# Retention with the value weights last: decayed scores times modulated rows, then the value projection; context keys of two heads ahead of the heads

## The chip, the cores and the metric

The kernel runs on one core of one Trainium2 chip. Its time is in device microseconds (us), the median over several executions of the same program. One more execution of each kernel was profiled; the rows and stretches below are from that one. Engines: PE is TensorE (matrix products; PEld its weight loads), DVE is VectorE, ACT is ScalarE, POOL is GpSimd, SP issues most of the DMAs. Each engine works through its own instructions strictly in program order.

## What is computed

A backbone of two layers over 256 latent tokens and 256 context tokens of width 1024. Layer 0 mixes tokens with a Fourier and neighbourhood-attention mixer, layer 1 with bidirectional retention; each layer ends in a mixture of experts. The change is in layer 1's retention, which reads (cut to what matters):

```python
xm = rmsnorm(x, g) * (1 + scale) + shift         # latent rows, "modulated"; cm the same for the context rows
q, k, v, g = split(xm @ w_in)                    # 4 heads: q and k 256 wide (k / 16, both with rotary), v and g 512 wide
kc, vc = split(cm @ w_in)                        # the context gives keys and values, without rotary
o = (decay * (q @ concat(kc, k).T)) @ concat(vc, v)     # both directions of the scan together: a full decay matrix
y = (silu(g) * rmsnorm(o)) @ w_out               # norm over the 512 columns of a head
```

With X the 512 modulated rows (context, then latent), P the decayed scores and Wv a head's value weights, a head's output is P (X Wv). It may also be computed as (P X) Wv.

## The kernel before, in words

Every float32 product is done in three products of a reduced format: each operand is split into a high part (a copy by ScalarE, names ending in hi or h) and a low part (a subtraction by VectorE, names ending in lo or l), and `mm3` (L313 to L320) adds high times high, low times high and high times low in one PSUM accumulator. Weights are split the same way: a load fills a tile `raw` (128x2048), `split` (L166 to L180) makes two `whi` on ScalarE (L176) and two `wlo` on VectorE (L178) from it. Raw tiles and pairs of whi and wlo come from two rings of slots, `raw` and `hl`; a load waits on its queue until its slot has been read. Loads go out on SP's queue, some small ones on GpSimd's.

Layer 1's retention begins in `moe0_tail`, behind the last expert of layer 0. `combine` adds the experts' sums to the residual rows `h`; `norm_scale` and `norm_mod` norm a tile of 128 rows, transpose it on TensorE (`nT`) and modulate it into `r_xc` (context) and `r_xl` (latent), features on the partitions. There the kernel loads head 0's value weights and key weights, computes the values of one context tile (`v_ps`) and the keys of the context for head 0 (`k_ps`).

`ret_heads` then goes through four heads. Per head: context keys (`k_ctx`), keys and queries of the latent tokens with rotary (`roped`, L1252 to L1254, tiles `qk_ps`, `rt`, `ro`), values of four token tiles (`v_ps`, 4 x 8 x 3 products of 512 columns), scores (`s_ps`, 24 products of 256 columns) times the decay (`pf`) and split (`ph`, `pl`), the gate (`g_ps`, 48 products of 512 columns, silu into `gt`), and the output (`ro_ps`, 2 x 4 x 3 products of 512 columns), normed and gated into `og`. Chunks of the conditioning (`ada_step`: a weight load, 64 small products into `ada_ps`, a bias into `adab`, and rows `mod` written to DRAM for later use) are spread between. Behind the heads `og` is transposed (`tsp`) and multiplied by the output weights (`ry_ps`).

The code is written in the order wanted; a scheduler then interleaves the engines' work, so that each engine's final order is not the code's.

Of the kernel before, what the change touches and what calls it, by code (L numbers as in the profile page):

```python
# [12 lines left out]
ALU = mybir.AluOpType  # L13
# [97 lines left out]
class Net:  # L111
    def __init__(self, ctx, tc, A, out, stop=None, dbg=None):
# [4 lines left out]
        self.add_slots(ctx, "raw", 4)  # L117
# [142 lines left out]
    def ada_mm(self, layer, c, aps, psp):  # L260
# [20 lines left out]
        def finish():  # L281
# [10 lines left out]
            if vec not in (SH1, SC1):  # L292
# [3 lines left out]
                for i in range(2 if layer == 0 else 1):  # L296
                    d = nc.gpsimd.dma_start(row[i, 512 * ch:512 * ch + 512].rearrange("(j p) -> j p", p=128), r[i:128:32])
# [24 lines left out]
    def norm_scale(self, t, x):  # L322
# [9 lines left out]
        return self.nc.vector.tensor_scalar(x, self.h[:, t], r, None, ALU.mult)  # L332
# [24 lines left out]
    def mixer0(self):  # L357
# [3 lines left out]
        with ExitStack() as es0:  # L361
# [142 lines left out]
            with ExitStack() as es:  # L504
# [4 lines left out]
                self.add_hl(self.ctx, 2, "right")  # L509
                self.hx = self.ctx.enter_context(ExitStack())  # L510
                self.add_raw(self.hx, 2)
# [225 lines left out]
    def moe0_tail(self, ep, psp, hps):  # L737
# [3 lines left out]
        self.kc = [xr.tile([128, 2, 256], F32R, name=f"r_kc{i}") for i in range(2)]  # L741
        self.v0 = xr.tile([128, 512], F32, name="r_v0")
# [3 lines left out]
        x = X["xg"]  # L746
        xms = lambda: ep.tile([128, 4, 128], F32, tag="g", name="xm")
        mm, add = self.combine(2)
        last = self.norm_scale(2, x[0])
# [3 lines left out]
        last = self.norm_scale(3, x[1])  # L753
        with after(last):
            self.ret_wv = wv = [self.weight(("ret_w_in", (), 4 * i, 4, 2048, 512)) for i in range(2)]
        for t in (2, 3):
            last = self.norm_mod(1, t, x[t - 2], xms, psp, *self.xc)
        with after(last):
            self.ret_w0 = w0 = self.weight(self.ret_keys(0)[0])
# [10 lines left out]
    def vproj(self, ws, x, t, ps):  # L770
        tk = slice(128 * t, 128 * t + 128)
        for k in range(8):
            self.mm3(ps, (x[0][:, k, tk], x[1][:, k, tk]), self.wk(ws[k // 4], k % 4), k == 0, k == 7)
        return ps

    def proj_t(self, w, x, ps, tk):
        for f in range(2):
# [8 lines left out]
    def k_ctx(self, w, ps, tk):  # L786
        self.proj_t(w, self.xc, ps, tk)
        self.split_scaled(self.kc[0][:, :, tk], self.kc[1][:, :, tk], ps[:, :, tk], 0.0625)
# [374 lines left out]
    def retention(self):  # L1163
        nc, A, tc = self.nc, self.A, self.tc
        h = self.h
        with ExitStack() as es:
# [4 lines left out]
            with ExitStack() as es1:  # L1171
                ogp = self.pool(es1, "r_og", 1)
                og = ogp.tile([128, 2, 2048], F32, name="og")
                with ExitStack() as es2:
# [4 lines left out]
                    self.ret_heads(wk, mmp, sp, psp, aps, xs, og)  # L1179
# [3 lines left out]
                self.hx = self.ctx.enter_context(ExitStack())  # L1183
                self.add_raw(self.hx, 3, late=True)
# [4 lines left out]
                for kc in range(4):  # L1189
                    oh, ol = xs[kc // 2]  # L1190
                    ks = slice(4 * (kc % 2), 4 * (kc % 2) + 4)
                    for t in range(2):
                        tq = slice(128 * t, 128 * t + 128)
                        self.transpose_split(og[:, t, 512 * kc:512 * kc + 512], 4, oh[:, ks, tq], ol[:, ks, tq], psp)
# [32 lines left out]
    def ret_heads(self, wk, mmp, sp, psp, aps, xs, og):  # L1227
# [5 lines left out]
        full, half = slice(0, 256), (slice(0, 64), slice(64, 128))  # L1233

        def proj(ws, t, name):
            ps = mmp.tile([128, 512], F32, tag="mm", name=name)
            tk = slice(128 * (t % 2), 128 * (t % 2) + 128)
            xhi, xlo = xs[t // 2]
            for k in range(8):
                self.mm3(ps, (xhi[:, k, tk], xlo[:, k, tk]), self.wk(ws[k // 4], k % 4), k == 0, k == 7)  # L1240
            return ps

        def weights(c0, pool=0):
            return [self.weight(("ret_w_in", (), 4 * i, 4, c0, 512), pool) for i in range(2)]
# [472 lines left out]
```

## Time and profile before

| | before |
|---|---|
| median of 3 executions | 1287.11 us (1286.89 to 1289.53) |
| profiled execution, its time | 1290.84 us |
| its span in the trace | 1289.0 us |
| TensorE busy | 1203.7 us, 93% |
| VectorE busy | 941.8 us, 73% |
| ScalarE busy | 755.6 us, 59% |

The busy shares are means over the whole program. The four heads lie between about 681 us and 909 us of the span, the norms ahead of them between about 641 us and 685 us, the start of layer 0's expert stage between about 325 us and 352 us.

### The profile page before, as it was taken

The page shows a single profiled execution, that of the slowest core. Times are in us where ns is not written, and L with a number is a line of the kernel's source. Part 1 is how long each engine was busy: PE and PEld are TensorE (multiplying, and loading weights), DVE is VectorE, ACT ScalarE, POOL GpSimd, SP SyncE. Part 2 cuts the span into 40 slices and gives each one's busy share as a digit, 9 for nine tenths or more (in the row PEclk, how much of TensorE's full clock was granted, in tenths as well). Part 3 has the DMA queues.
Part 4 walks back from the last instruction along what each step waited for, and adds up shares of the span by engine and source line. Part 5 has one row for each costly group of instructions (what it writes and reads, how often), then busy time and mean ns, then how long its engine had stood idle before and what let it go on. Part 6 is the DMA issues. An engine that isn't in the chain of part 4 may idle for free. (4 is left out here: it accounts for less than half of the span.)

```text
span 1289.0 us, 18819 instructions
## 1 busy us (share of the span) xinstructions
PE 1203.7 (93%) x7093; PEld 946.8 (73%) x7093; DVE 941.8 (73%) x1601; ACT 755.6 (59%) x1122; POOL 124.5 (10%) x126
## 2 busy tenths in 40 slices
PE   4999999898699999999979999999997999999995
PEld 3777666566588888777668888898776788877673
DVE  4755666866698989888897554554657899888985
ACT  3753555723488888778544433343435777777663
POOL 1010102300111112111000000000004000000020
PEclk8999999999799999999989999999998999999998
DMA  9666774342899999999883445432749999889980
GB/s 348 254 238 244 270 256 153 106 166 102 332 354 373 365 363 365 359 362 347 299 326 111 147 157 199 154 119 98 270 174 359 369 369 367 336 334 344 336 335 9
DMA packets 60885, 340.60 MB, mean 264 GB/s; under 512 B 10252, under 2 KB 14860, under 8 KB 24144
## 3 DMA queue, kind: packets, MB, share of 16 engines
q1 hardware_dynamic: 46656, 303.07, 62.4%
q0 software_dynamic: 11392, 31.81, 7.6%
q10 hardware_dynamic: 2736, 4.41, 1.0%
q8 instruction: 59, 0.97, 0.3%
q14 instruction: 42, 0.34, 0.1%
HBM read 333.74 MB, written 18.40 MB: 273 GB/s over the span
## 5 line engine op out<-in xcount | busy, mean ns | idle before, releaser
L178 DVE TENSOR_TENSOR wlo<-raw,whi 128x1024 fp32r<-128x1024 f32 x471 | 558.8, 1221 | 114.2 <-ACT whi L176 113.0
L176 ACT ACTIVATE whi<-raw 128x1024 fp32r<-128x1024 f32 x476 | 481.2, 1054 | 106.8 <-PE qk_ps L319 24.5
L319 PE MATMUL h_ps<-wlo,xh 128*128 128x512 f32 x512 | 208.6, 407 | 4.5 <-DVE wlo L178 4.3
L318 PE MATMUL h_ps<-whi,xh 128*128 128x512 f32 x512 | 206.1, 403 | 3.3 <-ACT xh L1457 2.4
L320 PE MATMUL h_ps<-whi,xl 128*128 128x512 f32 x512 | 206.1, 402 | 0.1
L319 PEld LDWEIGHTS h_ps<-wlo,xh 128*128 128x128 f32 x512 | 97.6, 191 | 38.4 <-DVE wlo L178 17.6
L318 PEld LDWEIGHTS h_ps<-whi,xh 128*128 128x128 f32 x512 | 97.9, 191 | 26.0 <-ACT xh L1457 2.6
L320 PEld LDWEIGHTS h_ps<-whi,xl 128*128 128x128 f32 x512 | 97.6, 191 | 21.3 <-DVE xl L675 0.7
L275 PE MATMUL ada_ps<-raw,cT 128*32 128x128 f32 x1536 | 53.8, 276 | 2.1 <-DMA raw<-in_ada_w 2.1
L319 PE MATMUL y_ps<-wlo,gh 128*128 128x512 f32 (+1 forms) x136 | 53.5, 394 | 0.4 <-DVE wlo L178 0.3
L318 PE MATMUL y_ps<-whi,gh 128*128 128x512 f32 (+1 forms) x136 | 53.0, 391 | 0.7 <-ACT gh L674 0.7
L320 PE MATMUL y_ps<-whi,gl 128*128 128x512 f32 (+1 forms) x136 | 52.6, 395 | 0.1
L275 PEld LDWEIGHTS ada_ps<-raw,cT 128*32 128x32 f32 x1536 | 41.4, 110 | 13.9 <-issue 9.2
L319 PE MATMUL y<-wlo,gh 128*128 128x512 f32 x124 | 49.1, 396 | 0.4 <-DVE wlo L178 0.3
L318 PE MATMUL y<-whi,gh 128*128 128x512 f32 x124 | 49.2, 397 | 0.2 <-ACT gh L674 0.2
L320 PE MATMUL y<-whi,gl 128*128 128x512 f32 x124 | 48.4, 400 | 0.9 <-DVE gl L675 0.8
L1104 POOL DMA_INDIRECT moe_sum<-y,tok x15 | 28.1, 1877 | 158.1 <-ACT y L1099 158.1
L674 ACT ACTIVATE gh<-tsp 128x512 fp32r<-128x512 f32 x32 | 19.1, 596 | 41.4 <-PE tsp L671 41.2
L318 PE MATMUL qk_ps<-xhi,whi 128*128 128x512 f32 x96 | 39.4, 410 | 0.0
L319 PE MATMUL qk_ps<-xlo,whi 128*128 128x512 f32 x96 | 38.7, 403 | 0.0
L320 PE MATMUL qk_ps<-xhi,wlo 128*128 128x512 f32 x96 | 38.3, 399 | 0.0
L1604 POOL DMA_INDIRECT out_dram<-hg,tok x4 | 10.6, 2638 | 268.0 <-DVE hg L1598 218.4
(441 smaller groups left out, 2391.9 us busy)
## 6 DMA issues: line engine op xcount, KB each, us to landing
raw<-in_moe_w SPq DMA_DIRECT2D x188, 1024.0 KB, 7.6
raw<-in_ada_w SPq DMA_DIRECT2D x48, 1024.0 KB, 5.3
raw<-in_ret_w_in SPq DMA_DIRECT2D x24, 1024.0 KB, 5.7
raw<-in_mixab_w_in SPq DMA_DIRECT2D x10, 1024.0 KB, 5.6
raw<-in_ret_w_out SPq DMA_DIRECT2D x8, 1024.0 KB, 4.9
raw<-in_mixab_w_out SPq DMA_DIRECT2D x4, 1024.0 KB, 8.2
raw<-in_moe_w POOLq DMA_DIRECT2D x4, 1024.0 KB, 11.0
bias<-in_rpb ACTq DMA_DIRECT2D x12, 256.0 KB, 5.6
```

The costliest lines, as they stand in the source:

```text
L176: self.nc.scalar.activation(hi, r, AF.Copy)
L178: eng.tensor_tensor(lo, r, hi.bitcast(F32), ALU.subtract)
L275: mm = nc.tensor.matmul(ps[32 * j:32 * j + 32, 0:128], self.cT[:, kk, :], raw[:, k, 128 * j:128 * j + 128], start=(kk == 0), stop=(kk == 7 ...
L318: mm(out, lh, rh, start=first, stop=False)
L319: mm(out, lh, rl, start=False, stop=False)
L320: self.mm_last = mm(out, ll, rh, start=False, stop=last)
L674: i = nc.scalar.activation(hi[:, b0:b0 + w], tv, AF.Copy)
L1104: nc.gpsimd.indirect_dma_start(out=self.F[:, :], out_offset=bass.IndirectOffsetOnAxis(ap=R["tok"][:, e:e + 1], axis=0), in_=y, in_offset=N ...
L1604: self.nc.gpsimd.indirect_dma_start(out=self.out[:, :], out_offset=bass.IndirectOffsetOnAxis(ap=idx, axis=0), in_=x, in_offset=None, bound ...
```

## The change

A head now computes Z = P X first (transposed, features on the partitions: `z_ps`, 8 blocks of 128 features x 4 token tiles x 3 products of 256 columns), splits it (`zh`, `zl`) and multiplies it by the value weights (`ro_ps`, 2 x 8 x 3 products of 512 columns). For this the modulated rows are needed with tokens on the partitions: `natural` multiplies each of the four tiles of normed rows by the scale row and adds the shift row, copies the high part (`xnh`) and subtracts for the low part. Those rows come by four broadcast loads from DRAM (`rows`), so the shift and scale of layer 1 are written to DRAM as well, by eight more small DMAs.

Around this: `moe0_tail` loads the key weights of heads 0 and 1 in place of head 0's value and key weights, and computes the context keys of head 0 and of half of head 1 (256 columns each product); the other half follows in `ret_heads` behind the latent norms. There are two sets of context keys. The gate is computed ahead of the scores and its silu goes to `og`; the next head's keys are computed between a head's scores and its Z. One conditioning chunk runs in each head (before, one in head 0's stretch of code and up to two in the others). The rings are smaller in the heads: three raw tiles and four hl pairs, where there were four and six. The fourth raw tile holds the low part of the natural context rows until the last Z.

```diff
@@ the end of a conditioning chunk
-            if vec not in (SH1, SC1):
+            if layer or vec not in (SH1, SC1):
...
-                for i in range(2 if layer == 0 else 1):
+                for i in range(2 if layer == 0 or vec in (SH1, SC1) else 1):
@@ moe0_tail
-            self.ret_wv = wv = [self.weight(("ret_w_in", (), 4 * i, 4, 2048, 512)) for i in range(2)]
+            self.ret_w0 = w = [self.weight(self.ret_keys(0)[0])]
...
-            self.ret_w0 = w0 = self.weight(self.ret_keys(0)[0])
+            w.append(self.weight(self.ret_keys(1)[0]))
...
-        v = hps.tile([128, 512], F32, tag="h", name="v_ps")
-        self.vproj(wv, self.xc, 0, v)
-        nc.scalar.copy(self.v0, v)
-        self.k_ctx(w0, hps.tile([128, 2, 256], F32, tag="h", name="k_ps"), slice(0, 256))
+        self.k_ctx(0, w[0], hps.tile([128, 2, 256], F32, tag="h", name="k_ps"))
+        self.k_ctx(1, w[1], hps.tile([128, 2, 256], F32, tag="h", name="k_ps"), (0,))
@@ ret_heads, ahead of the loop over heads
+        xnh = wk.tile([128, 4, D], F32R, name="xnh")
+        self.ring["raw"][:] = [q for q in self.ring["raw"] if q is not self.raw1]
+        xc = self.raw1.tile([128, 2, D], F32R, tag="raw", name="xnlc")
...
+        def rows(i):
+            t = self.raw_tile()
+            for j, vec in enumerate((SC1, SH1)):
+                nc.gpsimd.dma_start(t[:, 1024 * j:1024 * j + 1024],
+                                    self.modrow[1, vec][i:i + 1].partition_broadcast(128))
+            return t
+        def natural(m, x, r, tmp=None):
+            V.tensor_tensor(x, x, r[:, 0:D], ALU.mult)
+            V.tensor_tensor(x, x, r[:, D:], ALU.add)
+            nc.scalar.activation(xnh[:, m], x, AF.Copy)
+            V.tensor_tensor(xnl[m], x, xnh[:, m].bitcast(F32), ALU.subtract)
...
+        self.k_ctx(1, self.ret_w0[1], mmp.tile([128, 2, 256], F32, tag="mm", name="k_ps"), (1,))
+        kl = keys(0, self.ret_w0[0])
+        with self.tc.issue_after(last.ins):
+            r = rows(1), rows(0)
+            for m in range(4):
+                natural(m, h[:, 2 + m] if m < 2 else x[m - 2], r[m // 2])
@@ ret_heads, in a head
-                w_v = weights(2048 + 512 * hd)
-                for m in range(4):
-                    vproj(w_v, m)
+            if hd < 3:
+                w = self.weight(self.ret_keys(hd + 1)[0])
+                if hd:
+                    self.k_ctx(hd + 1, w, mmp.tile([128, 2, 256], F32, tag="mm", name="k_ps"))
+                kl = keys(hd + 1, w)
+            def z_part(i):
+                z = mmp.tile([128, 2, 256], F32, tag="mm", name="z_ps")
+                for b in range(2):
+                    cs = kcol(2 * i + b, 128)
+                    for m in range(4):
+                        self.mm3(z[:, b], (xnh[:, m, cs], xnl[m][:, cs]), (ph[:, m], pl[:, m]), m == 0, m == 3)
...
+            w_v = weights(2048 + 512 * hd)
+            o = [sp.tile([128, 512], F32, tag="s", name="ro_ps") for t in range(2)]
+            z_part(0)
+            for i in range(4):
+                if i < 3:
+                    z_part(i + 1)
+                for b in range(2):
+                    k = 2 * i + b
+                    for t in range(2):
+                        tq = kcol(t, 128)
+                        self.mm3(o[t], (zh[i][:, b, tq], zl[i][:, b, tq]), self.wk(w_v[k // 4], k % 4), k == 0, k == 7)
```

How this moves instructions is seen in each engine's order of the built program. First VectorE at head 0, before: the last split of latent rows (`r_xl`), value splits (`vl`), weight splits, and the rotary of the keys.

```order
L351 TENSOR_SCALAR og<-nT,modcol 128x128 x3
L354 TENSOR_TENSOR r_xl_13258<-og,r_xl_13257 128x4x128 x2
L1262 TENSOR_TENSOR vl<-v_ps,vh 128x512
L178 TENSOR_TENSOR wlo<-raw,whi 128x1024 x3
L1262 TENSOR_TENSOR vl<-v_ps,vh 128x512
L178 TENSOR_TENSOR wlo<-raw,whi 128x1024 x2
L1252 TENSOR_TENSOR rt<-qk_ps,ropet 64x512 x2
L1253 TENSOR_TENSOR ro<-qk_ps,ropet 128x512
L178 TENSOR_TENSOR wlo<-raw,whi 128x1024
L1254 TENSOR_TENSOR ro<-ro,rt 128x512
L178 TENSOR_TENSOR wlo<-raw,whi 128x1024
L784 SCALAR_TENSOR_TENSOR k_13447<-ro,k_13446 128x512
```

The same place now. Ahead of these rows stand the last split of latent rows, two scale operations (L1246) and two shift operations (L1247) of the context rows, one scale operation of latent rows, and the keys' rotary with two low parts (L1249) between its steps; the first `wlo` here belongs to head 0's gate weight, the last row is the queries' split.

```order
L777 SCALAR_TENSOR_TENSOR k_13402<-ro,k_13401 128x512
L1247 TENSOR_TENSOR xn<-xn,raw 128x1024
L1246 TENSOR_TENSOR xn<-xn,raw 128x1024
L1257 TENSOR_TENSOR rt<-qk_ps,ropet 64x512
L1249 TENSOR_TENSOR xnl_13284<-xn,xnh 128x1024
L1247 TENSOR_TENSOR xn<-xn,raw 128x1024
L1257 TENSOR_TENSOR rt<-qk_ps,ropet 64x512
L1258 TENSOR_TENSOR ro<-qk_ps,ropet 128x512
L1249 TENSOR_TENSOR xnl_13285<-xn,xnh 128x1024
L1259 TENSOR_TENSOR ro<-ro,rt 128x512
L180 TENSOR_TENSOR wlo<-raw,whi 128x1024
L777 SCALAR_TENSOR_TENSOR q_13483<-ro,q_13482 128x512
```

All twelve operations of `natural` (four each of L1246, L1247 and L1249) now stand between the last split of latent rows and the first split of a gate weight.

Second, GpSimd's queue at the start of layer 0's experts, before: row broadcasts and row writes of the stage ahead of it, then the gather of the first expert's rows (`xg`), four weight loads, and the second gather.

```order
L312 DMA g_3528<-mod_5_1752 128x1024
L312 DMA g_3530<-mod_5_1752 128x1024
L892 DMA xd_2322<-xm_3265 128x1024
L1713 BRANCH_PREFETCH_HINT
L1026 DMA xg_3540<-xd_2322,tok_3471 128x1024
L157 DMA raw<-in_moe_w 128x2048 x4
L1026 DMA xg_3541<-xd_2322,tok_3471 128x1024
L710 TENSOR_LOAD ovi_3512
```

The same place now:

```order
L314 DMA g_3541<-mod_5_1755 128x1024
L314 DMA g_3543<-mod_5_1755 128x1024
L887 DMA xd_2330<-xm_3273 128x1024
L1734 BRANCH_PREFETCH_HINT
L1021 DMA xg_3553<-xd_2330,tok_3479 128x1024
L299 DMA mod_0_3527<-adab 4x128 x4
L159 DMA raw<-in_moe_w 128x2048 x4
L1021 DMA xg_3554<-xd_2330,tok_3479 128x1024
L712 TENSOR_LOAD ovi_3520
L1108 COMPARE_AND_BRANCH
```

Four writes of `mod` rows (`L299`) have come between the first gather and the four weight loads.

Third, ScalarE at the end of the heads, before: silu of head 3's gate, weight copies (the `whi` there belong to the gate), the copies and squares of the output, and the copies of transposed rows for the output product.

```order
L1314 ACTIVATE gt<-g_ps 128x512
L176 ACTIVATE whi<-raw 128x1024 x3
L1314 ACTIVATE gt<-g_ps 128x512
L176 ACTIVATE whi<-raw 128x1024
L1322 COPY og<-ro_ps 128x512
L1324 ACTIVATE jk,r_ss<-og 128x512
L1322 COPY og<-ro_ps 128x512
L1324 ACTIVATE jk,r_ss<-og 128x512
L674 ACTIVATE r_xl_13257<-tsp 128x4x128 x4
L674 ACTIVATE r_oc_15400<-tsp 128x4x128 x2
```

The same place now; the two `whi` nearest to the squares (L1343) are those of the first output weights, the ones that `ry_ps` needs first.

```order
L1326 ACTIVATE zh<-z_ps 128x512 x2
L178 ACTIVATE whi<-raw 128x1024
L1326 ACTIVATE zh<-z_ps 128x512
L178 ACTIVATE whi<-raw 128x1024
L1326 ACTIVATE zh<-z_ps 128x512
L178 ACTIVATE whi<-raw 128x1024 x2
L1343 ACTIVATE jk,r_ss<-ro_ps 128x512
L178 ACTIVATE whi<-raw 128x1024
L1343 ACTIVATE jk,r_ss<-ro_ps 128x512
L676 ACTIVATE r_xl_13263<-tsp 128x4x128 x2
L178 ACTIVATE whi<-raw 128x1024
L676 ACTIVATE r_xl_13263<-tsp 128x4x128 x2
```

The copies of the output (L1322) are gone, and two weight copies stand ahead of and between the squares.

## Rows read from the trace of the kernel before

**Rows 1.** The page, part 1: busy us and share of the span.

```profile
PE 1203.7 (93%) x7093; PEld 946.8 (73%) x7093; DVE 941.8 (73%) x1601; ACT 755.6 (59%) x1122; POOL 124.5 (10%) x126
```

**Rows 2.** Windows: length, busy us PE, PEld, DVE, ACT, POOL; clock; DMA; GB/s.

```profile
700.00:740.00 40.00, 39.72 (x311) 35.66 (x310) 25.87 (x46) 15.12 (x22) 1.13 (x2) 1.00 0.40 137
...
860.00:910.00 50.00, 49.74 (x271) 41.98 (x269) 26.40 (x31) 20.58 (x27) 0.95 (x1) 1.00 0.35 123
```

**Rows 3.** Timeline of PE at the heads' start: start, duration, instruction.

```profile
662.13 0.28 PE L318 MATMUL k_ps<-r_xc,whi 128*128 128x256 f32 x1
...
665.36 0.28 PE L318 MATMUL k_ps<-r_xc,whi 128*128 128x256 f32 x1
...
668.04 1.95 PE L275 MATMUL ada_ps<-raw,cT 128*32 128x128 f32 x64
...
673.09 0.40 PE L318 MATMUL v_ps<-whi,r_xc 128*128 128x512 f32 x1
...
677.06 0.39 PE L320 MATMUL v_ps<-whi,r_xc 128*128 128x512 f32 x1
...
681.44 0.50 PE L318 MATMUL v_ps<-whi,r_xl 128*128 128x512 f32 x1
```

**Rows 4.** Tile ro_ps: ns min/median/max, first and last start us.

```profile
L320 PE MATMUL ro_ps<-vh,pl x32: 388/389/397, 719.5 to 908.6; 128*128 128x512 f32 x32
```

**Rows 5.** Tile k_ps: weight loads of its 256-column products.

```profile
L318 PEld LDWEIGHTS k_ps<-r_xc,whi x64: 187/188/192, 660.8 to 855.1; 128*128 128x128 f32 x64
```

**Rows 6.** Timeline of DVE, norms and head 0 (idle before, in brackets).

```profile
660.64 2.35 DVE L178 TENSOR_TENSOR wlo<-raw,whi 128x1024 fp32r<-128x1024 f32 x2
...
683.67 1.30 DVE L354 TENSOR_TENSOR r_xl<-og,r_xl 128x512 fp32r<-128x512 f32 x2 [0.47 <-ACT r_xl L353]
688.34 0.69 DVE L1262 TENSOR_TENSOR vl<-v_ps,vh 128x512 fp32r<-128x512 f32 x1 [3.37 <-ACT vh L1261]
...
699.84 1.39 DVE L1252 TENSOR_TENSOR rt<-qk_ps,ropet 64x512 f32<-64x512 f32 x2
```

**Rows 7.** Timeline of ACT, third pair of weight copies.

```profile
655.09 2.01 ACT L176 ACTIVATE whi<-raw 128x1024 fp32r<-128x1024 f32 x2
```

**Rows 8.** Timeline of PE, start of the first expert stage.

```profile
331.10 1.94 PE L671 MATMUL tsp<-cst,xg 128*128 128x128 f32 x8 [5.44 <-DVE mk L728]
...
348.79 0.37 PE L1018 MATMUL tbw<-wv,os 128*128 128x48 bf16 x8 [2.91 <-DVE wv L985]
```

**Rows 9.** Windows at the first expert stage, columns as rows 2.

```profile
324.00:326.00 2.00, 0.73 (x2) 0.37 (x2) 1.28 (x7) 0.66 (x2) 0.52 (x1) 0.50 0.00 0
...
332.00:336.00 4.00, 4.00 (x12) 2.70 (x11) 4.00 (x8) 3.09 (x4) 0.00 (x0) 0.51 1.02 414
336.00:340.00 4.00, 4.00 (x19) 3.24 (x18) 4.00 (x10) 2.01 (x2) 0.00 (x0) 1.00 1.01 424
```

**Rows 10.** Tile mod: the issues that write it, ns min/median/max.

```profile
L297 POOL DMA_DIRECT2D mod<-adab x24: 537/542/652, 74.4 to 974.9; - x24
```

**Rows 11.** Timeline of POOL, start of the first expert stage.

```profile
326.57 2.17 POOL L157 DMA_DIRECT2D raw<-in_moe_w  x4
```

**Rows 12.** Timeline of ACT, start of the first expert stage.

```profile
343.37 1.06 ACT L176 ACTIVATE whi<-raw 128x1024 fp32r<-128x1024 f32 x1 [4.68 <-DMA raw<-in_moe_w]
```

**Rows 13.** Timeline of SP's queue towards the end of the heads.

```profile
865.58 27.57 SPq L157 DMA_DIRECT2D raw<-in_ret_w_out  x4
```

**Rows 14.** The page, part 6: KB each, us to landing.

```profile
raw<-in_ret_w_out SPq DMA_DIRECT2D x8, 1024.0 KB, 4.9
```

**Rows 15.** Timeline of ACT at the end of the heads.

```profile
908.99 0.58 ACT L1322 COPY og<-ro_ps 128x512 f32<-128x512 f32 x1 [1.38 <-PE ro_ps L320]
909.61 0.63 ACT L1324 ACTIVATE jk<-og 128x512 f32<-128x512 f32 x1
910.14 0.19 ACT L1324 ACTIVATION_READ_ACCUMULATOR jk<-og 128x1 f32 x1
910.71 1.08 ACT L674 ACTIVATE r_xl<-tsp 128x512 fp32r<-128x512 f32 x2 [0.37 <-PE tsp L671]
```

More of the change, by code (lines that the diff above doesn't have):

```diff
@@ L320, in mm3, with norm_scale @@
         self.mm_last = mm(out, ll, rh, start=False, stop=last)
-    def norm_scale(self, t, x):
+    def norm_scale(self, t, x, out=None):
         nc = self.nc
@@ L740, in moe0_tail @@
         self.xc = [xr.tile([128, 8, 256], F32R, name=f"r_xc{i}") for i in range(2)]
-        self.kc = [xr.tile([128, 2, 256], F32R, name=f"r_kc{i}") for i in range(2)]
-        self.v0 = xr.tile([128, 512], F32, name="r_v0")
+        self.kc = [[xr.tile([128, 2, 256], F32R, name=f"r_kc{j}{i}") for i in range(2)] for j in range(2)]
         self.ada_q = [(1, c) for c in (6, 7, 8, 9)]
@@ L1233, in ret_heads, with weights @@
         full, half = slice(0, 256), (slice(0, 64), slice(64, 128))
[L1235 to L1244, printed above, removed]
+        kcol = lambda t, n=512: slice(n * t, n * t + n)
+        xnh = wk.tile([128, 4, D], F32R, name="xnh")
+        self.ring["raw"][:] = [q for q in self.ring["raw"] if q is not self.raw1]
+        xc = self.raw1.tile([128, 2, D], F32R, tag="raw", name="xnlc")
+        xnl = [xc[:, 0], xc[:, 1]] + [wk.tile([128, D], F32R, name=f"xnl{t}") for t in range(2)]
+        def weights(c0):
+            return [self.weight(("ret_w_in", (), 4 * i, 4, c0, 512)) for i in range(2)]
+        def rows(i):
[9 more added lines that the diff above has]
+            V.tensor_tensor(xnl[m], x, xnh[:, m].bitcast(F32), ALU.subtract)
         def roped(w, out, scale):
@@ new lines, in keys @@
+        def keys(hd, w):
+            kl = [wk.tile([128, 2, 256], F32R, tag=f"k{i}", name=f"k{i}") for i in range(2)]
+            roped(w, kl, 0.0625)
+            return kl
+        x = [ogp.tile([128, D], F32, tag=f"g{t}", name="xn") for t in range(2)]
+        xm = [ogp.tile([128, 2, 4, 128], F32, tag=f"g{t}", name="xm") for t in (2, 3)]
+        xm = [xm[i // 2][:, i % 2] for i in range(4)]
+        for t in range(2):
+            self.norm_scale(t, x[t])
+        for t in range(2):
+            last = self.norm_mod(1, t, x[t], lambda: xm.pop(0), psp, *xs[0])
@@ L1290, in ret_heads @@
             nc.gpsimd.dma_start(dm, self.dmat[hd].rearrange("p (m q) -> p m q", m=4))
-            if hd:
-                w_v = weights(2048 + 512 * hd)
-                for m in range(4):
-                    vproj(w_v, m)
+            ws = weights(4096 + 512 * hd)
+            ps = [mmp.tile([128, 512], F32, tag="mm", name="g_ps") for t in range(2)]
+            for k in range(8):
+                for t in range(2):
+                    tq = kcol(t, 128)
+                    self.mm3(ps[t], (xs[0][0][:, k, tq], xs[0][1][:, k, tq]), self.wk(ws[k // 4], k % 4), k == 0, k == 7)
+            og.append(ogp.tile([128, 2, 512], F32, tag=f"g{hd}", name="og"))
+            for t in range(2):
+                nc.scalar.activation(og[hd][:, t], ps[t], AF.Silu)
             ph = wk.tile([128, 4, 256], F32R, tag="ph", name="ph")
@@ L1310, in ret_heads @@
             self.ada_step(aps, psp)
-            gt = wk.tile([128, 2, 512], F32, tag="gt", name="gt")
-            ws = weights(4096 + 512 * hd)
-            for t in range(2):
-                nc.scalar.activation(gt[:, t], proj(ws, t, "g_ps"), AF.Silu)
+            if hd < 3:
[3 more added lines that the diff above has]
+                kl = keys(hd + 1, w)
+            zh, zl = [], []
```

93 lines of the change are left out of this document (34 added, 59 removed).

## The prediction, made before the changed kernel was run

> **What bounds the kernel now.** I read the engine shares first, then the stretches of the four heads, then the single engines around the start of the heads, because an average over the program says nothing of the place that the change touches. TensorE is busy for 93% of the span, VectorE for 73% [rows 1]. In the heads TensorE has no gaps to speak of: 39.72 of 40 us, and 49.74 of 50 us at their end, at the full clock, while VectorE has a third to a half of its time free [rows 2]. There a product saved on TensorE is time saved, and VectorE's extra work is free as long as TensorE has products queued that don't wait for it. At the first head that condition is what must be looked at: before it lies a chain of norms on VectorE, and TensorE gets the latent rows from that chain.
>
> **Products.** A product of 512 columns follows the one before it after (677.06 - 673.09) / 17 = 0.2335 us, one of 256 columns after (665.36 - 662.13) / 27 = 0.1196 us, a conditioning chunk takes 1.95 us [rows 3]. Per head the change takes out 96 + 24 products of 512 and adds 96 of 256 and 48 of 512: 4 x (28.0 - 22.7) = 21.3 us less. Not all of it counts. In the kernel before, head 0's context value products (48 of 512) lie inside the norm chain, where TensorE waits anyway; now context keys of head 1 lie there. So I count only what stands behind the first product on latent rows. Before: 624 x 0.2335 + 624 x 0.1196 + 3 x 1.95 = 226.2 us, from 681.44 [rows 3] to 907.6; the last product of the heads starts at 908.6 in the trace [rows 4], so the count is good to 1 us. Now: 384 x 0.2335 + 960 x 0.1196 + 4 x 1.95 = 212.3 us. **Term A: -13.9.**
>
> Two prices could spoil A. A 256-column product carries as many weight loads as one of 512, and a load takes 188 ns, longer than 0.1196 us [rows 5]. If loads set the pace, A would be 384 x 0.2335 + 960 x 0.188 + 7.8 less 624 x 0.2335 + 624 x 0.188 + 5.9, that is +9.1 us. But the 0.1196 us was measured with a load before every product, so they overlap and I take it. The Trainium skill, page "TensorE: Matmul & The Clock Gate", section "Back-to-back issue gap", says that spacing is set by load and product together, and gives about 131 ns at 512 columns and 81 ns at 128. By an estimate on the line between these, 256 columns cost 98 ns, three quarters of 512, and the change would save nothing on products; this trace, with a ratio of 0.51, differs.
>
> **Start of the heads.** The last split of latent rows ends at 683.67 + 1.30 = 684.97 [rows 6]. Ahead of it the change takes two weight copies out of ScalarE that stand between the copies of the context rows (2.01 us at 655.09, with the last two row copies behind them [rows 7]), and one pair of weight splits out of VectorE (2.35 us at 660.64 [rows 6]). I let the chain come 2.0 us earlier; bounds 0 (the row broadcasts and the second weight load share the DMA and land late) and 4 (both pairs count). Into the chain come one weight split (1.18) and the rest of the split keys (0.35), and two value splits leave (0.65 each): +0.2. Latent rows are complete at 683.2. The first product is now a key product over both token tiles; it needs the second tile's first half, 0.65 earlier, 682.5, where 681.44 sufficed before. **Term B: +1.1** (-1.5 to +3.1).
>
> **The row operations of head 0.** Behind that split VectorE has, in its order, twelve operations of 128x1024 and both rope chains before the first gate weight is split; before the change nothing but weight and value splits and ropes stood there, and it idled 3.37 us [rows 6]. A 128x1024 operation costs 2.35 / 2 = 1.18 us, the rope's first two 1.39 together, each later step, of 128x512, about 0.65 (0.69 alone at 688.34) [rows 6]. So 12 x 1.18 + (1.39 + 3 x 0.65) + (1.39 + 2 x 0.65) + 1.18 = 21.4 us: the gate weight is ready at 704.6. TensorE has keys and queries for 96 x 0.1196 = 11.5 us, to 694.0, and the third gate product then waits; scores and the next head's keys are queued behind it. **Term C: a stall of +10.6** (8, if some operations hide in waits that I count twice, to 13, if the keys run at the low clock and hold the rope back). Row copies on ScalarE and the gate load (its slot is free from the query weight's split) are in time.
>
> **Clock.** After such a stall products are slow: after 5.44 us without a product at 331.10 [rows 8] TensorE started 12 products in 332 to 336 at 0.51 of the clock and 19 in the next 4 us at 1.00 [rows 9]. That is 7 products lost, 7 x 0.2335 = 1.6, a little more with the two us ahead of it. **Term D: +2.0** (0.5 to 3).
>
> **The first expert stage.** The layer's shift and scale are now also written to DRAM: four more issues stand on GpSimd's queue between the first row gather and the four loads of expert weights, 0.54 us each [rows 10]. Those loads go out at 326.57 [rows 11] into a DMA that is idle (0.00 in 324 to 326) and full a little later (1.02 in 332 to 336, 1.01 in 336 to 340) [rows 9]. ScalarE waits 4.68 us for one of them until 343.37 [rows 12], and TensorE idles 2.91 us through it [rows 8]. Nothing covers a later start. **Term E: +2.2** (0 if another load than these was the late one, 3 at most). The other four issues lie in mixer 0, where VectorE and TensorE don't wait for GpSimd: 0.
>
> **End of the heads.** Before, the first four loads of the output weight are issued from 865.58 on [rows 13], long ahead. Now the first one gets the slot lent to the low part of the context rows, free only with the last modulated-row product, some 24 x 0.2335 + 6 x 0.1196 = 6.3 us before the end. It lands 4.9 us later [rows 14], 1.4 before the end, and its two copies (1.0 each [rows 7]) stand among ScalarE's two squares (0.63 + 0.19 each): the row copy comes -1.4 + 2 x 1.0 + 2 x 0.82 = 2.2 us after the end instead of 910.71 - 908.99 = 1.7 [rows 15]. With a landing somewhat later than the median, **term F: +1.0** (0 to 2.5).
>
> Edits that I cost at nothing: ring and slot sizes, the order of gate and scores, the output kept in PSUM, norms in place. Their cover is TensorE's queue in heads 1 to 3, where each split is due some 3 us before its product; where that fails a load's landing becomes the wait (a rival below).
>
> **Sum.** -13.9 + 1.1 + 10.6 + 2.0 + 2.2 + 1.0 = +3.0. The profiled execution takes 1290.84 us (1.84 of it outside the span), so 1293.8 for one like it; against the median of 1287.11, 3.7 below it, 1290.1. About 0.2%, 2.6 us, is what a measurement here can tell from no change.
>
> **Rivals.**
> - The norm chain comes forward by more than 5.5 us beyond my 2: without 48 value products of 0.2335 = 11.2 us between them, the combining products (which VectorE's chain waits for) may run earlier. For it: TensorE is in use there. Against: VectorE is busy without a pause from 660.64 on. At 7 us more the time is 1283; a stall that does not come at all (-12.6) would give 1277.5. It decides from 5.6 us on; chance 0.23.
> - The same, by 1.5 to 5.5 us, or a stall at its lower bound: no change that can be told, 1286. Chance 0.11.
> - The smaller rings bind: three weight slots and four split slots in heads 1 to 3 where there were four and six. A load is then issued only when a split frees its slot, lands 4.9 us later and is copied and split behind that; 2 us of waiting in each of three heads gives 1296. VectorE's and the DMA's free time [rows 2] speak against it. Chance 0.15.
> - Weight loads set the pace of 256-column products (+23 against my sum, 1313): chance 0.01, since 0.1196 us was measured.
>
> My sum with its ordinary errors keeps 0.50; its own range is 1286 to 1294, of which 0.22 counts as no change and 0.28 as slower. Together: faster 0.23, same 0.33, slower 0.44. The range runs from 1281 (most of the first rival) to 1297 (most of the third).
>
> **What would show it.** Right: in the trace after, no latent value products, 0.12 us between modulated-row products; a TensorE gap of 8 to 13 us ended by the first gate-weight split, with twelve 128x1024 operations ahead of it on VectorE, then some microseconds at the low clock; the expert loads 2.2 us later behind the gather, and TensorE's gap there 5 us instead of 2.91; from the first latent product to the last of the heads about 225 us. Wrong: if that gap is under 5 us (rows done earlier, or gate weights split ahead of them), if a DMA or a slot ends the waits in heads 1 to 3, or if the heads' first product starts before 678.

## The result, and the profile after the change

The changed kernel takes 1295.34 us (median of 4 runs, 1293.24 to 1297.16), the kernel before 1287.31 on the same chip (4 runs): a ratio of 1.0053, 95% interval 1.0041 to 1.0066. It is slower, by 0.5%. The profiled execution took 1293.24 us, the fastest of its four; that of before, 1290.84, lies above all four that were timed, so the two traces show less than the medians do.

The page of the kernel after, busy time by engine, beside [rows 1]:

```profile
PE 1184.4 (92%) x7189; PEld 942.0 (73%) x7189; DVE 956.5 (74%) x1616; ACT 755.8 (59%) x1120; POOL 132.8 (10%) x138
```

TensorE is busy 19 us less, and the kernel is longer. So the products were saved, and more than that was lost in waits. Some waits of TensorE after the change, the costliest first (engine, tile, line, who ended them: us in all, times, longest; the one left out between the first two, 8.0 us at the transposes of a later norm, was 7.9 before):

```profile
PE s_ps L320 <- ACT q L776: 8.8, 1, 8.8
...
PE tbw L1013 <- DVE wv L980: 7.1, 1, 7.1
...
PE h_ps L320 <- PEq L1634: 4.8, 1, 4.8
...
PE qk_ps L320 <- ACT r_xl L355: 2.8, 1, 2.8
```

The first and the second shown lie at the two places that the prediction spoke of; of before, the second was 2.91 us [rows 8]. Windows over the start of head 0, and then the stretches of [rows 2] (length, busy us of PE, PEld, DVE, ACT, POOL, granted clock, DMA share, GB/s):

```profile
690.00:696.00 6.00, 6.00 (x53) 6.00 (x52) 5.21 (x7) 3.54 (x5) 0.00 (x0) 1.00 0.41 165
696.00:706.00 10.00, 1.18 (x7) 0.74 (x5) 9.89 (x12) 4.01 (x5) 0.00 (x0) 0.71 0.30 105
706.00:712.00 6.00, 6.00 (x19) 4.77 (x19) 4.01 (x5) 0.00 (x0) 0.00 (x0) 0.63 0.53 187
700.00:740.00 40.00, 34.12 (x255) 30.11 (x256) 24.67 (x30) 12.95 (x16) 1.12 (x2) 0.87 0.61 225
...
780.00:820.00 40.00, 40.00 (x271) 36.93 (x270) 22.17 (x38) 13.43 (x19) 0.00 (x0) 1.00 0.35 128
820.00:860.00 40.00, 39.79 (x333) 37.06 (x332) 19.68 (x25) 14.10 (x18) 1.12 (x2) 1.00 0.46 175
860.00:910.00 50.00, 49.99 (x353) 44.15 (x352) 26.58 (x44) 19.04 (x26) 1.51 (x2) 1.00 0.49 182
```

In 696 to 706 TensorE works 1.18 us of ten and VectorE 9.89. Behind it TensorE is busy without a gap, but at a clock of 0.63, with 19 products in 6 us. From 740 on nothing waits. TensorE's timeline there (start, duration, instruction, idle time ahead in brackets):

```profile
682.80 0.79 PE L320 MATMUL qk_ps<-r_xl,whi 128*128 128x256 f32 x2 [2.77 <-ACT r_xl L355]
...
683.90 0.41 PE L322 MATMUL qk_ps<-r_xl,wlo 128*128 128x256 f32 x1
684.12 0.41 PE L320 MATMUL qk_ps<-r_xl,whi 128*128 128x256 f32 x1
684.33 0.41 PE L321 MATMUL qk_ps<-r_xl,whi 128*128 128x256 f32 x1
684.54 0.41 PE L322 MATMUL qk_ps<-r_xl,wlo 128*128 128x256 f32 x1
...
696.14 0.63 PE L320 MATMUL g_ps<-whi,r_xl 128*128 128x512 f32 x2
705.59 0.58 PE L320 MATMUL s_ps<-q,r_kc 128*128 128x256 f32 x1 [8.82 <-ACT q L776]
705.97 0.42 PE L320 MATMUL s_ps<-q,k 128*128 128x256 f32 x1
706.18 0.67 PE L321 MATMUL g_ps<-wlo,r_xl 128*128 128x512 f32 x1
706.65 0.63 PE L322 MATMUL g_ps<-whi,r_xl 128*128 128x512 f32 x1
...
710.49 0.39 PE L320 MATMUL g_ps<-whi,r_xl 128*128 128x512 f32 x1
```

Keys and queries run, and two gate products with the high part of the weight follow. Next in TensorE's order stand two score products, which need the high part of the queries, and then the gate product that needs the low part of the weight. TensorE goes on after 8.82 us, when ScalarE has copied the queries:

```profile
704.90 0.63 ACT L776 ACTIVATE q<-ro 128x512 fp32r<-128x512 f32 x1 [2.11 <-DVE ro L1259]
```

That copy waited for VectorE's last step of the rotary (704.18), and the weight's split follows on VectorE directly behind it (704.79). VectorE's timeline over that stretch shows what stood ahead of both; of before it had idle time at the start of head 0 [rows 6]:

```profile
683.99 2.35 DVE L1246 TENSOR_TENSOR h<-h,raw 128x1024 f32<-128x1024 f32 x2
686.26 2.35 DVE L1247 TENSOR_TENSOR h<-h,raw 128x1024 f32<-128x1024 f32 x2
...
699.35 1.23 DVE L1249 TENSOR_TENSOR xnl<-xn,xnh 128x1024 fp32r<-128x1024 f32 x1
700.49 1.22 DVE L1247 TENSOR_TENSOR xn<-xn,raw 128x1024 f32<-128x1024 f32 x1
...
703.05 1.22 DVE L1249 TENSOR_TENSOR xnl<-xn,xnh 128x1024 fp32r<-128x1024 f32 x1
704.18 0.69 DVE L1259 TENSOR_TENSOR ro<-ro,rt 128x512 f32<-128x512 f32 x1
704.79 1.22 DVE L180 TENSOR_TENSOR wlo<-raw,whi 128x1024 fp32r<-128x1024 f32 x1
```

The split is done at 706.0; the prediction said 704.6. So the same row operations hold back the queries and the gate weight: without the two score products, TensorE would have waited to 706.0 instead of 705.6. GpSimd at the first expert stage, before (with the gather that stands ahead of [rows 11]) and after:

```profile
325.48 1.08 POOL L1026 DMA_INDIRECT xg<-xd,tok  x1 [8.41 <-DVE adab L283]
326.57 2.17 POOL L157 DMA_DIRECT2D raw<-in_moe_w  x4
...
322.68 1.09 POOL L1021 DMA_INDIRECT xg<-xd,tok  x1 [8.39 <-DVE adab L285]
323.76 2.22 POOL L299 DMA_DIRECT2D mod<-adab  x4
325.97 1.64 POOL L159 DMA_DIRECT2D raw<-in_moe_w  x3
328.32 0.53 POOL L159 DMA_DIRECT2D raw<-in_moe_w  x1 [0.71 <-issue]
```

Four row writes stand between the gather and the loads. ScalarE's and TensorE's wait for it, beside [rows 12] and [rows 8]: 6.91 us (of before 4.68), and 7.05 (2.91), each up to the same place. From the timelines of ScalarE and TensorE:

```profile
343.67 1.06 ACT L178 ACTIVATE whi<-raw 128x1024 fp32r<-128x1024 f32 x1 [6.91 <-DMA raw<-in_moe_w]
349.09 0.50 PE L1013 MATMUL tbw<-wv,os 128*128 128x48 bf16 x8 [7.05 <-DVE wv L980]
```

By stages, after less before, from starts in the two timelines: up to the first gather 322.68 - 325.48 = -2.8 (the kernel before has a spread there too, experiment 8); from it to TensorE's resumption at tile tbw 26.4 - 23.3 = +3.1; then to the transposes of the first context rows -0.7; from there to the first product on latent rows 36.3 - 34.6 = +1.7; from that to the last product of the heads 227.4 - 227.1 = +0.3; to the first product of the second expert stage 73.2 - 70.3 = +2.9; from there to the end -2.1. Together, but for rounding, +2.4, the difference of the spans.

### The profile page after: what moved, and what is told of

It is laid out like the page before. It is cut to its first block, busy times and chain, and to the rows that moved or that the text cites. A ratio compares the mean times of both kernels' runs of the same rounds, so it can differ in the third digit from the quotient of the medians.

```text
span 1291.4 us, 19066 instructions
## 1 busy us (share of the span) xinstructions
PE 1184.4 (92%) x7189; PEld 942.0 (73%) x7189; DVE 956.5 (74%) x1616; ACT 755.8 (59%) x1120; POOL 132.8 (10%) x138
## 5 line engine op out<-in xcount | busy, mean ns | idle before, releaser
L320 PE MATMUL qk_ps<-r_xl,whi 128*128 128x256 f32 x128 | 37.0, 291 | 2.8 <-ACT r_xl L355 2.8
```

The costliest lines, as they stand in the source:

```text
L320: mm(out, lh, rh, start=first, stop=False)
```

## The experiments

All were timed in five rounds against the kernel before on the same chip. 0 to 3 ran on one chip, 4 to 6, 7 to 9, and 10 and 11 on others, where the kernel before took 1289.15, 1288.40, 1288.35 and 1287.48 us; so ratios, and not medians, compare kernels of different groups. "Heads" is the time from the first product on latent rows to the last product of the heads, "experts" that from the first row gather to TensorE's resumption, both in the profiled execution.

| kernel | median us | ratio to before | interval | heads | experts |
|---|---|---|---|---|---|
| before (8) | 1287.52 | 0.9999 | 0.9984 to 1.0014 | 227.1 | 23.6 |
| changed (0) | 1293.69 | 1.0042 | 1.0027 to 1.0057 | 227.6 | 26.5 |
| 1 | 1288.37 | 0.9992 | 0.9983 to 1.0002 | 221.8 | 26.5 |
| 2 | 1291.74 | 1.0023 | 1.0013 to 1.0033 | 227.4 | 24.6 |
| 3 | 1285.68 | 0.9978 | 0.9964 to 0.9991 | 222.1 | 24.7 |
| 4 | 1293.42 | 1.0044 | 1.0030 to 1.0057 | 227.2 | 26.4 |
| 5 | 1283.73 | 0.9974 | 0.9959 to 0.9988 | 219.4 | 24.4 |
| 6 | 1293.97 | 1.0054 | 1.0035 to 1.0072 | 229.7 | 24.2 |
| 7 | 1288.37 | 0.9996 | 0.9984 to 1.0008 | 228.1 | 23.4 |
| 9 | 1282.91 | 0.9956 | 0.9942 to 0.9970 | 219.6 | 24.5 |
| 10 | 1279.91 | 0.9937 | 0.9923 to 0.9952 | 217.4 | 24.0 |
| 11 (as 9) | 1282.70 | 0.9962 | 0.9947 to 0.9977 | 219.5 | 24.1 |

**Theory after the first trace:** two places cost the gain, VectorE's row operations ahead of the first gate split, and the four writes ahead of the expert loads. Rivals: the stall is the gate weight's load or TensorE's own order; the smaller rings cost the rest.

**0. The changed kernel again**, as the partner of 1 to 3.

> The changed kernel once more, beside the others, so that they can be compared with it on the same chip. Both theories: 1295 us, ratio to the kernel before about 1.005; the profile shows again a TensorE gap of about 9 us behind head 0's queries and of about 7 us at the first expert stage. If it comes out within 0.2% of the kernel before, the loss is not of the kernel and the rest has to be read against this run.

It gave 1293.69, ratio 1.0042. By the ratios the cost lies at 5.4 us by this, 6.8 by the first measurement; the intervals overlap.

**1. The latent tiles' row operations behind head 0's scores**, six of the twelve in the code (the tiles `x` and `xm` also change places, so that `x` stays until then; so in 3, 5, 6 and 9 to 11):

```diff
-            for m in range(4):
-                natural(m, h[:, 2 + m] if m < 2 else x[m - 2], r[m // 2])
+            for m in range(2):
+                natural(m, h[:, 2 + m], r[0])
...
+            if hd == 0:
+                for m in (2, 3):
+                    natural(m, x[m - 2], r[1])
```

> One part undone: the natural rows of the two latent tiles are made behind head 0's scores, not ahead of its gate weights (seven 128x1024 operations stand ahead of the first gate weight's split, not twelve). Theory 1 (VectorE's row operations hold TensorE back): the split comes 5 x 1.18 = 5.9 us earlier, TensorE's gap there falls from 9 us to about 3, and most of the low-clock stretch behind it goes, so 6 to 8 us faster than the changed kernel, about 1288. Theory 2 (time is lost in many places, by the smaller rings and more traffic): the operations come back as a wait for the low parts ahead of Z, and the time stays within 2 us of the changed kernel.

5.3 us less than the changed kernel by the medians, 6.4 by the ratios. In the trace the stall is 2.86 us instead of 8.82, 5.96 less, and the heads are 5.8 us shorter. From the timelines of VectorE and TensorE:

```profile
690.07 1.22 DVE L1246 TENSOR_TENSOR xn<-xn,raw 128x1024 f32<-128x1024 f32 x1
...
701.89 0.50 PE L321 MATMUL g_ps<-wlo,r_xl 128*128 128x512 f32 x1 [2.86 <-DVE wlo L180]
```

The scheduler left one of the six, the scale of a latent tile, ahead of the gate weight's split, so five operations went from there, and 5 x 1.18 = 5.9. Here the score products stand behind the gate, and the split itself ends the wait. The stall follows the row operations; a late load would have kept it.

**2. The four writes on SP's queue instead of GpSimd's**:

```diff
-                    d = nc.gpsimd.dma_start(row[i, 512 * ch:512 * ch + 512].rearrange("(j p) -> j p", p=128), r[i:128:32])
+                    q = nc.sync if vec == SH1 else nc.gpsimd
+                    d = q.dma_start(row[i, 512 * ch:512 * ch + 512].rearrange("(j p) -> j p", p=128), r[i:128:32])
```

> One part undone: the four writes of layer 1's shift rows go out on SP's queue and no longer stand on GpSimd's queue ahead of the expert weight loads. Theory 1: the loads follow the gather at once as before the change, TensorE's gap at the first expert stage falls from 7 us to about 3 to 4, and the kernel is 2 to 3 us faster than the changed one, about 1292.5. Theory 2 (the DMA is full there anyway and only the order of landing changes, or a later wait takes it back): within 1 us of the changed kernel.

2.0 us less, and 1.9 in the trace from gather to resumption. TensorE's gap is 3.51 us, and in GpSimd's timeline of 2 the loads follow the gather at once:

```profile
324.54 1.08 POOL L1022 DMA_INDIRECT xg<-xd,tok  x1 [8.40 <-DVE adab L285]
325.63 2.16 POOL L159 DMA_DIRECT2D raw<-in_moe_w  x4
```

About 1 us of the 3 stays: in the seven kernels with these writes on SP's queue the stretch takes 24.0 to 24.7 us, in the three traces without any writes there 23.3 to 23.6. What holds it was not tried.

**3. Both together.**

> Both of these edits together. Theory 1: the two waits lie 340 us apart and add up, 8 to 11 us faster than the changed kernel, about 1285.5, ratio to the kernel before 0.997 to 1.000. Theory 2: as the changed kernel, 1.005.

1285.68, 8.0 us less than the changed kernel, where the two alone gave 5.3 and 2.0: they add up. This is faster than the kernel before. What is left of the stall is 2.88 us ahead of the third gate product, with some ten gate products 0.43 us apart behind it. From TensorE's timeline of 3:

```profile
698.07 0.50 PE L322 MATMUL g_ps<-wlo,r_xl 128*128 128x512 f32 x1 [2.88 <-DVE wlo L180]
```

**4. The writes alone, in the kernel before**: only the condition that sends the layer-1 shift and scale to DRAM too.

```diff
-            if vec not in (SH1, SC1):
+            if layer or vec not in (SH1, SC1):
...
-                for i in range(2 if layer == 0 else 1):
+                for i in range(2 if layer == 0 or vec in (SH1, SC1) else 1):
```

> The kernel before, with only the extra writes of the layer-1 shift and scale to DRAM (four of them between the first row gather and the four expert weight loads on GpSimd's queue). Theory: the loads start 2.2 us later, TensorE's gap ahead of the first expert stage grows from 2.9 to 5 to 6 us, and the time grows by 2 to 3 us (ratio 1.0015 to 1.0025). Rival: the delay seen after the change came from the smaller weight rings or another order of loads there; then the gap stays near 2.9 us and the ratio at 1.000.

TensorE's gap went to 7.23 us (before 2.91 and, in the second trace, 4.49), and gather to resumption to 26.4, as in the changed kernel (26.4 and 26.5). So rings and order of loads have no part in it. But the time rose by 5.0 us (interval 3.9 to 7.3), more than the 3.0 that the trace shows at this place. GpSimd's and TensorE's timelines, now of the kernel before with this part alone:

```profile
326.74 2.22 POOL L297 DMA_DIRECT2D mod<-adab  x4
328.95 1.64 POOL L157 DMA_DIRECT2D raw<-in_moe_w  x3
331.15 0.54 POOL L157 DMA_DIRECT2D raw<-in_moe_w  x1 [0.55 <-issue]
...
352.00 0.50 PE L1018 MATMUL tbw<-wv,os 128*128 128x48 bf16 x8 [7.23 <-DVE wv L985]
```

**5. As 3, and the two low-part subtractions of the context rows behind head 0's query split:**

```diff
             nc.scalar.activation(xnh[:, m], x, AF.Copy)
-            V.tensor_tensor(xnl[m], x, xnh[:, m].bitcast(F32), ALU.subtract)
+            if m > 1:
+                low(m, x)
...
+            if hd == 0:
+                with self.tc.issue_after(q_last.ins):
+                    for m in range(2):
+                        low(m, h[:, 2 + m])
```

> As e3_both, and the two low-part subtractions of the context rows moved behind head 0's query split. Theory: the first gate weight splits come earlier on VectorE, the remaining wait of 2.9 us at the gate products goes and with it the products at the low clock (2 us); VectorE has 3.5 us free between 706 and 712 us, so 3.5 to 4.9 us less than e3_both. If the cost of the change was the stall and the expert loads, this kernel is 8 to 9 us faster than the kernel before; the products alone should give 13.9 less 1.1, 0.5, 1 and the 1.6 us of keys at the low clock. Rival: the wait moves to the next keys (their weight split is behind the moved rows); then the time is that of e3_both.

The gate products no longer wait, and no product there runs at the low clock; but 2.3 us of it come back at the next keys, half the rival's case. TensorE's timeline there:

```profile
710.72 0.33 PE L291 MATMUL ada_tp<-cst,adab 128*128 128x128 f32 x1 [0.58 <-DVE adab L285]
712.76 0.39 PE L321 MATMUL qk_ps<-r_xl,whi 128*128 128x256 f32 x1 [1.71 <-ACT whi L178]
```

The heads are 2.7 us shorter than in 3, the median 1.95, the ratio hardly (0.9974 beside 0.9978): the sign is shown in the trace, not by the times. Both sizes that I expected were missed: 3.5 to 4.9 less than 3, and 8 to 9 less than the kernel before, where the ratio gives 3.4. So the stall and the expert loads are not the whole cost (the missing term below).

**6. As 3, but all twelve row operations behind head 0's scores.**

> As e3_both, but all twelve row operations behind head 0's scores, ahead of the split of head 1's key weight. Theory: it is VectorE's order and not the gate weight's load; no wait at head 0's gate products, and a wait of 10 to 12 us at head 1's key products instead, ended by VectorE's weight split, with about 2 us at the low clock behind it; 7 to 10 us slower than e3_both, so like e2_rows_by_sp or slower. Rival: TensorE's queue or the load set the stall; then the gate products still wait about 3 us and the time is that of e3_both.

At head 0's gate products 0.25 us of waiting is left, and the time is 8.3 us more than 3 by the medians, 9.8 by the ratios, as expected. The 10.4 us of waiting came in two pieces (timelines of TensorE and of SP's queue):

```profile
716.40 1.93 PE L277 MATMUL ada_ps<-raw,cT 128*32 128x128 f32 x32 [5.15 <-DMA raw<-in_ada_w]
723.59 0.47 PE L291 MATMUL ada_tp<-cst,adab 128*128 128x128 f32 x1 [5.25 <-DVE adab L285]
...
711.32 0.33 SPq L159 DMA_DIRECT2D raw<-in_ada_w  x1
```

I had expected the wait to end with head 1's weight split. It ended earlier in the order, at the conditioning chunk: once at its load, once at its small addition, which stood among the row operations on VectorE. The place moved with the row operations and the size nearly stayed: that is the theory. The load was late for its slot: it was issued at 711.32, behind the chunk's own first products, which end at 711.25 (in 3 both loads of the chunk went out before them, at 699.8 and 702.7). The broadcast rows hold two of the three raw slots until the row operations have read them, and the next weight load, at 717.68, was released by one of these (`h`, L1248). So late row operations cost twice, on VectorE and in the ring.

**7 and 8. The writes of the scale alone in the kernel before, and the kernel before again.** In 7 the four writes of the shift are left out, and the condition of experiment 4 reads

```diff
+            if (layer and vec != SH1) or vec not in (SH1, SC1):
```

> The kernel before, with only the extra writes of the layer-1 scale, which go out in mixer 0 at about 183 and 199 us on GpSimd's queue; the shift's four, which stand ahead of the expert loads, are left out. Writes of both cost 5.0 us in e4_before_rows, where the trace showed 2.2 at the expert stage. Theory A, the prediction's: the writes in mixer 0 cost nothing; the ratio is within 0.999 to 1.001, and most of e4's 5 us lie at the expert stage in the runs that have no trace. Theory B: they cost the missing 2 to 3 us (ratio 1.0015 to 1.0025), with a wait in mixer 0 between 180 and 320 us that the kernel before hasn't.

> The kernel before, unchanged, for a second trace of it: ratio 1.000 (0.9988 to 1.0012). If the 2.5 us that its first profiled execution lay above the median were lost ahead of the first row gather (325.48 us there, 322.4 to 324.5 in the kernels with the change), the gather comes at 322 to 324 us here, with a span of 1285 to 1287; if it comes at 325 us again, the change made mixer 0 faster.

7 shows no change (0.9996, with an interval of 1.5 us to either side): no cost of the writes in mixer 0 is seen, as predicted. So the 5 us of experiment 4 belong to the shift's four writes, or to them and chance: 3.0 are seen at the expert stage (the 2.2 in the expectation is the predicted size), the other 2 (0.9 to 4.3 by the interval) in no place of the one trace taken there; they stay open. The second trace of before has a span of 1286.5 with the gather at 324.89, 0.6 us earlier than the first, so most of the 2.5 us between the two was not lost there, and the -2.8 us ahead of the gather is not settled as a gain: across the kernels with the change it comes between 322.05 and 325.68.

**9. As 5, with the scale's writes on SP too.**

> As e5_lows_behind, with the four scale writes in mixer 0 on SP's queue too. Theory B of e7: 2 to 3 us less than e5_lows_behind, about 1281. Theory A: no change (1282.5 to 1285), or 1 to 2 us more if the writes on SP hold back the weight loads that stand behind them there.

Ratio 0.9956 and, in 11, 0.9962; 5 had 0.9974. The intervals overlap: no difference is shown, and 7 speaks against one.

**10 and 11. As 9, with 60 products that nobody reads in TensorE's waits for the latent rows' norm**, and 9 again beside it.

```diff
+        def fill(n, i):
+            with self.tc.issue_after(i.ins):
+                for j in range(n):
+                    nc.tensor.matmul(fps[:, 0:256], self.wk(self.ret_w0[1], j % 8, slice(0, 128))[0],
+                                     self.xc[0][:, j % 8], start=True, stop=True)
...
+        fill(16, self.mm_last)
         for t in range(2):
             last = self.norm_mod(1, t, x[t], lambda: xm.pop(0), psp, *xs[0])
+            fill((22, 22)[t], self.tp_last)
```

> As e9_all_by_sp, with 60 more products of 256 columns that nobody reads, on TensorE in its waits for the norm of the latent rows (16 ahead of the first tile's transposes, 22 behind them, 22 behind the second tile's). Theory: the first 17 key products ran at the low clock because TensorE waited ahead of them; with the waits filled they follow each other after 0.12 us instead of 0.21, 1.6 us less behind the first latent product, and the first key product comes no later than before; 1.0 to 2.0 us less than the same kernel without the filling, with the granted clock at 1.00 from 670 to 690 us. Rival: the low clock there has another cause than the waits; then the key products keep their 0.21 us and the time stays, or grows by up to 1 us where the filling holds up transposes.

> e9_all_by_sp once more, as the partner of e10_filled on the same chip: ratio to the kernel before 0.9956, as there (0.9942 to 0.9970).

1279.91 beside 1282.70: 2.8 us less, more than the 1.0 to 2.0 expected, the best time of all. Windows of 10, columns as above, and the transposes of the second latent tile:

```profile
670.00:680.00 10.00, 9.61 (x81) 9.40 (x82) 9.65 (x36) 5.67 (x16) 0.00 (x0) 1.00 0.19 57
680.00:690.00 10.00, 8.77 (x72) 8.32 (x70) 10.00 (x14) 7.29 (x11) 0.00 (x0) 1.00 0.01 2
...
678.83 1.07 PE L346 MATMUL nT<-cst,xn 128*128 128x128 f32 x8
```

and of 11:

```profile
670.00:680.00 10.00, 4.75 (x31) 3.96 (x30) 9.82 (x38) 6.17 (x14) 0.00 (x0) 0.82 0.09 36
680.00:690.00 10.00, 7.62 (x47) 7.40 (x48) 8.26 (x9) 4.36 (x9) 0.00 (x0) 0.67 0.37 118
...
677.67 1.94 PE L346 MATMUL nT<-cst,xn 128*128 128x128 f32 x8 [2.93 <-DVE xn L335]
```

With the waits filled the clock stays at 1.00 and the key products follow each other after 0.12 us. From the transposes of the first context rows to the end of the heads the trace takes 252.6 us instead of 255.8: 1.1 of it ahead of the first latent product, 2.1 in the heads. The low clock came from the waits. That all of the 2.8 us comes from the clock is not shown, because the built programs differ in more than the filling. In the code of 10 half of head 1's context keys moved ahead of the norms (on TensorE they ran there in 11 too), and the scheduler changed VectorE's and ScalarE's order: in 11 two weight splits stand in the norm chain (673.56 and 680.08), in 10 two row operations of a latent tile stand there (678.60 and 682.21), and the splits behind it. What the clock gives back can be read by itself: the transposes above take 0.9 us less, the 384 key and query products 46.8 us instead of 48.1, waits left out, together 2.2 of the 3.2 us. What limits 10 next is VectorE: query products wait 1.57 us for a weight split, one of those that came later.

## Why the prediction was right in its sign, and short in its size

It said 1290.1, slower, range 1281 to 1297; the kernel is slower, inside the range, and the sum of +3.0 us came out as +5.4 and +6.8 by the ratios. By its own steps:

- **A, products, -13.9: right.** From the starts in the timeline after, 384 modulated-row products take 46.3 us (0.1205 apart), 192 value products 45.1 (0.2347). The weight loads did not set the pace; the estimate of 98 ns that the prediction worked out from the Trainium skill ("TensorE: Matmul & The Clock Gate", "Back-to-back issue gap") was too low as well. Nothing in the heads from 740 on waits, so the rings rival is out too.
- **B, start of the heads, +1.1: +1.7** against the first trace of before, 2.6 against the second. The chain came forward about as said up to the first latent tile (the split of the key weight 2.5 us earlier on the clock, 658.14 instead of 660.64). The second tile's last split came only 0.9 earlier, and the first key product waits 2.77 us for ScalarE's copy of that tile's rows. That rules out the rival of a chain over 5.5 us earlier.
- **C, the stall, +10.6: mechanism right, 1.8 too long.** The gate split is ready at 706.0 instead of 704.6, and keys and queries ended at 696.1 instead of 694.0, which would make it 9.9. The two gate products ahead of the wait take 0.6 of that, and the score products, which the prediction had behind the gate, start 0.4 ahead of the split: so 8.82, and the wait ends with the queries' copy, not with the gate split as the prediction said. Both stand behind the row operations, and experiments 1, 3 and 6 move the wait with these.
- **D, gate products at the low clock, +2.0: right in size, by luck in its working.** Ten of them are 0.43 apart, 10 x 0.197 = 2.0. But the 12 products that the prediction read in 332 to 336 [rows 9] are not all of 512 columns: five are transposes that began at 331.10. Of products of 512 columns, six ran at the low clock, from 332.88 to 335.93, and lost 3.05 - 6 x 0.2335 = 1.65 us, the same 1.6.
- **The missing term.** The sum put keys and queries at 0.1196 us. The first of them ran at 0.21, since TensorE had waited for most of the time from 672 on. Beyond 0.1196 each, the 384 key and query products lost 2.5 us (of before 1.1), scores and the next heads' context keys 1.6 (of before nothing). So the heads came to +0.3 and not -13.9 + 10.6 + 2.0 = -1.3; that they miss by no more is partly luck, since C was 1.8 too long. The prediction had this as a bound of C only ("if the keys run at the low clock"), and not as a loss. For the keys and queries experiment 10 shows the cause, and gives back 1.3 us. The context keys' part (0.9 us of the 1.6) is there in 10 too; its cause is open.
- **E, the expert loads, +2.2: mis-sized, +3.0.** Experiment 4 has it alone. The sum counted four issues of 0.54; the trace has another 0.71 ahead of the last load, which takes its issue to 328.32, 5.6 behind the gather's start; of before it was 2.7 behind it.
- **F, end of the heads, +1.0: +0.5.** The row copy comes 912.88 - 910.62 = 2.3 us behind the last product, of before 1.7 [rows 15].
- **Not in the sum:** at the second expert stage TensorE waits 4.8 us for its own sequencer at a branch, of before 2.41 for ScalarE. It is there in the changed kernel and in 0 to 3, 5, 6, 9 and 11, from 3.3 to 4.8. In 10 and in 4 a gap of 3.5 and 3.6 us stands at the same place, but ended by ScalarE. Behind it the program takes 2.1 us less than before. The DMA engines are full around it in both kernels (1.02 in 974 to 978). Its cause is open, and it wasn't tried.

B (0.6 to 1.5), the heads (1.6), E (0.8 to 0.9), F (-0.5) and the branch with what follows (0.3) take +3.0 to between 5.8 and 6.8, near the 5.4 and 6.8 that were measured. This leaves out the stretch ahead of the first gather and the one from TensorE's resumption to the context rows' transposes, -2.8 and -0.7 in the first two traces: there traces of the kernel before differ by 0.6 and 1.1 among themselves.

## What to carry to other kernels

A change that trades products for elementwise work is paid where the elementwise work is queued: look at what stands behind it on its engine, and put it behind what TensorE waits for next. Here the same arithmetic is 0.4 to 0.5% slower or 0.6% faster than before by the order of twelve operations, the queue of a few small writes and a filled wait. When products behind a wait are costed, take the spacing at the low clock for the first ones, from a row that shows them.

## What the runs showed of the hardware that was not expected

- Sixty products that nobody reads, in TensorE's waits, kept the granted clock at 1.00, where it was 0.82 and 0.67 without them. The kernel with them is 2.8 us faster; 2.2 us of that is read in products that ran at the full clock, the rest is not separated from the changed order of VectorE.
- At the low clock a 256-column product follows the one before after 0.213 us (683.90 to 684.54, three products), at the full one after 0.1196 to 0.1205. The Trainium skill, page "TensorE: Matmul & The Clock Gate", section "Back-to-back issue gap", gives for a product by itself, without a budget for its weight load, columns / 1.2 GHz at the low level and columns / 2.4 GHz + 2.5 ns at the full one. By an estimate from it these are 213 and 109 ns for 256 columns. With the first the trace agrees, the second is exceeded by about 10%.
- Four small writes of 0.55 us each on GpSimd's queue delayed TensorE by 3.0 us (experiment 4), more than the sum of their issues; with them on SP's queue 0.4 to 1.4 us of it stays (experiments 2, 3, 5, 6 and 9 to 11).
